# Gated linear attention with its features on the partitions: decays, queries and keys come out of TensorE unturned, and the state is kept at the middle of each tile

## The chip, the cores and the metric

The kernel runs on one core of a Trainium2 chip. The metric is the device time of one execution in microseconds (us). Instructions run on five engines that each work through their own queue in order: TensorE (PE in the profile), VectorE (DVE), ScalarE (ACT), GpSimd (POOL) and SyncE (SP, which issues most transfers). They wait for each other through semaphores.

## The reference, cut to what matters

The program computes two blocks on 512 tokens of width 1024. The first block, of two layers, is the one that the change touches. Its layer projects the normalized input to everything that two attentions need, runs both, gates them and projects back:

```python
z = rmsnorm(x, norm_g[l]) @ w_in[l]
(g_q, g_k, g_v, g_lr, g_gate, c_q, c_kv, k_pe, m_gate) = split(z)
log_a = log_sigmoid(g_lr @ w_gla_gate_up[l] + b_gla_gate[l]) / 16     # 512 x 4 heads x 64
# gated linear attention, 4 heads, keys of 64 features, values of 128, chunks of 64 tokens
b = cumsum(log_a within the chunk)
q_dec, k_inv = q * 64**-0.5 * exp(b), k * exp(-b)
o = tril(q_dec @ k_inv.T) @ v + q_dec @ state
state = exp(b_last) * state + (k * exp(b_last - b)).T @ v
o_gla = rmsnorm(o) * silu(g_gate)
# o_mla: causal softmax attention of 4 heads, queries and keys of 128 + 64 (rotated) features
x = x + concat(o_gla, o_mla * silu(m_gate)) @ w_out[l]
```

The second block (another mixer and a feed-forward part) is not touched.

## The kernel before, in words

All of the state fits on the chip: 512 tokens are four tiles of 128, `t` = 0 to 3, and the input `u` lies with its features on the partitions. A large projection is a chain of 24 matmuls of 512 columns, three for each of eight slices of 128 features (`mm3`, L232 to L234: each operand is split into a high and a low part, and high by high, high by low and low by high are added). The splits of the weights are a ScalarE cast (L94) and a VectorE subtraction (L95). Small matmuls and transposes are in float32; such a matmul has two records in the trace, a transpose one.

A layer of the first block runs in this order: a narrow projection (latent queries and keys, gate inputs) with `post_a`, `post_b`, `post_c` behind it, tile by tile; `queries` and `decays` (the log gates `la`); `keys`; `attention`; `output`. Between these steps stand calls of `fill`. A `Fill` holds a list of generators, each a large projection cut into pieces of 12 matmuls: the values (`vfill`), then queries and keys of the linear attention, then the two gates. One call issues the next piece on TensorE and then runs what was put off with `later(d, fn)` for d calls. The fill calls are thus what keeps TensorE busy while VectorE, ScalarE and GpSimd work on small things, and the order of the calls sets the order of every engine's queue.

The linear attention of a tile goes through `gla_decay` (cumulative sums of `la` as two float32 matmuls of 256 columns, L611 and L612, chunk ends in L621, then exponentials), `gla_qk` (the projected tile, tokens on the partitions, times the exponentials, L630 to L634), `gla_turn` (four transposes bring queries and keys to features on the partitions, copied in L644; then the update of the state, L656, added in L663 on VectorE, and the state at the tile's middle by one GpSimd multiplication, L649), `gla_scores` (L674) and `gla_out` (L688, L694), each one fill call after the other. The two 64-row halves of L674, L694 and L724 are pairs whose matmuls stand side by side in TensorE's array.

Behind `gla_out` comes a normalization: ScalarE squares the result in its PSUM banks (L699), VectorE sums (L700) and adds the epsilon (L701), GpSimd takes the power of -1/2 (L246), and VectorE multiplies out of PSUM (L706, tile `og`). Only then are the two PSUM tiles free. They come from the pool `"s"` of three buffers, from which `gla_scores`, `gla_out`, `mla_scores` (L721, L724, two tiles for two heads) and `keys` take theirs in turn; `"z"` has two (projections), `"tr"` two (transposes and state updates), `"o"` one.

Of the kernel before, what the change touches and what calls it, by code (L numbers as in the profile page):

```python
# [18 lines left out]
P = 128  # L19
# [153 lines left out]
class Layer:  # L173


    def __init__(self):
        self.fill = Fill()
        self.rqs, self.gexp, self.state = [], {}, None
        self.o, self.th, self.parts, self.ready, self.lat = {}, {}, {}, set(), {}
        self.scored = False  # L180
        self.oz = []


class K:
# [102 lines left out]
    def later_constants(self):  # L287
# [3 lines left out]
        c = cst.tile([P, 4 * P + 3], F32, name="c128")  # L291
# [3 lines left out]
        self.u_cum = c[:, P:2 * P]  # L295
        self.u_suf = c[:, 2 * P:3 * P]
        self.cmask = c[:, 3 * P:4 * P]
        self.ones = c[:, 4 * P:4 * P + 1]
# [207 lines left out]
    def decays(self, L):  # L506

        nc = self.nc
        ex = self.big([P, NT, 256])
        for t in range(NT):  # L510
# [8 lines left out]
        nc.vector.tensor_tensor(L.la[:], L.la[:], ex[:], ALU.subtract)  # L519
# [45 lines left out]
    def keys(self, L, wkv, t):  # L565
# [5 lines left out]
        for b in range(2):  # L571
            z = self.psum("o" if b and t % 2 else "s")
# [35 lines left out]
    def gla_decay(self, L, t):  # L608
        nc = self.nc
        psb = self.psum("s")  # L610
        nc.tensor.matmul(psb[:, 0:256], self.u_cum, L.la[:, t, :], start=True, stop=True)  # L611
        nc.tensor.matmul(psb[:, 256:512], self.u_suf, L.la[:, t, :], start=True, stop=True)  # L612
        e = self.lay.tile([P, 3, 256], F32, tag="gexp", name=self.name("gexp"))
        nc.scalar.activation(e[:, 0, :], psb[:, 0:256], AF.Exp)
        nc.scalar.activation(e[:, 1, :], psb[:, 0:256], AF.Exp, scale=-1.0)
        nc.scalar.activation(e[:, 2, :], psb[:, 256:512], AF.Exp)
        L.gexp[t] = e
        if t:
            pd = self.psum("tr", (P, 2, 256))
            for pr in range(2):  # L620
                nc.tensor.matmul(pd[:, pr, 0:2], L.la[:, t, pr * P:(pr + 1) * P], self.ends,  # L621
                                 start=pr == 0, stop=pr == 1)
            nc.scalar.activation(L.dec[:, t, :, :], pd[:, :, 0:2], AF.Exp)

    def gla_qk(self, L, t, z):
        nc = self.nc
        e, r = L.gexp.pop(t), L.r
        q_ = self.t2()
        ke = self.lay.tile([P, 256], F32, tag="ke", name=self.name("ke"), bufs=2)
        nc.vector.scalar_tensor_tensor(q_[:, 0:256], z[:, 0:256], L.r8[:, t:t + 1], e[:, 0, :],  # L630
                                       ALU.mult, ALU.mult)
        nc.vector.scalar_tensor_tensor(q_[:, 256:512], z[:, 256:512], r[:, t:t + 1], e[:, 1, :],
                                       ALU.mult, ALU.mult)
        nc.vector.scalar_tensor_tensor(ke[:], z[:, 256:512], r[:, t:t + 1], e[:, 2, :],  # L634
                                       ALU.mult, ALU.mult)
        L.fill.later(1, lambda: self.gla_turn(L, t, q_, ke))

    def gla_turn(self, L, t, q_, ke):
        nc = self.nc
        pst = self.psum("tr", (P, 4, P))  # L640
        for c in range(4):
            self.transpose(pst[:, c, :], q_[:, c * P:(c + 1) * P])
        qkT = self.lay.tile([P, 4, P], F32, tag="qkT", name=self.name("qkT"), bufs=2)
        nc.scalar.copy(qkT[:], pst[:])  # L644

        st = None
        if t:
            st = self.lay.tile([P, 2, P], F32, tag="mid", name=self.name("mid"), bufs=2)
            nc.gpsimd.tensor_tensor(st[:], L.state[:],  # L649
                                    L.dec[:, t, :, 0:1].to_broadcast([P, 2, P]), ALU.mult)  # L650
        if t < NT - 1:
            pu = self.psum("tr", (P, 2, P))
            for i in range(2):
                for par in range(2):
                    h = 2 * i + par
                    nc.tensor.matmul(pu[64 * par:64 * par + 64, i, :], ke[:, h * 64:(h + 1) * 64],  # L656
                                     L.v[:, t, h * P:(h + 1) * P], start=True, stop=True)
            if t == 0:
                L.state = self.lay.tile([P, 2, P], F32, tag="state", name=self.name("st"))
                nc.vector.tensor_copy(L.state[:], pu[:])  # L660
            else:
                for pr in range(2):
                    nc.vector.scalar_tensor_tensor(L.state[:, pr, :], L.state[:, pr, :],  # L663
                                                   L.dec[:, t, pr, 1:2], pu[:, pr, :],
                                                   ALU.mult, ALU.add)
        L.fill.later(1, lambda: self.gla_scores(L, t, qkT, st))

    def gla_scores(self, L, t, qkT, st):
        nc = self.nc
# [10 lines left out]
        L.fill.later(1, lambda: self.gla_out(L, t, qkT, st))  # L680

    def gla_out(self, L, t, qkT, st):
        nc = self.nc
        po = [self.psum("s", (P, 4, P)), self.psum("s", (P, 4, P))]
        for i in range(2):
# [4 lines left out]
        if st is not None:  # L690
            for i in range(2):
                for par in range(2):
                    b = slice(64 * par, 64 * par + 64)
                    nc.tensor.matmul(po[par][:, i, :], qkT[b, i, :], st[b, i, :],  # L694
                                     start=False, stop=i == 1)
        og = self.lay.tile([P, 4, P], F32, tag="o", name=self.name("og"), bufs=4)
# [153 lines left out]
    def layer(self, l):  # L850
# [11 lines left out]
        L.la = self.lay.tile([P, NT, 256], F32, tag="la", name=self.name("la"))  # L862
# [58 lines left out]
        L.r8, L.rh = self.sm(NT), self.sm(NT)  # L921
        nc.vector.tensor_scalar(L.r8[:], L.r[:], GLA_DK ** -0.5, None, ALU.mult)
# [12 lines left out]
        fill()  # L935
        for t in range(1, NT):
# [4 lines left out]
        L.dec = self.lay.tile([P, NT, 2, 2], F32, tag="dec", name=self.name("dec"))  # L941
        fill.add(self.tok_fill(T, lambda t, z: self.gla_qk(L, t, z),
                               lambda t: self.gla_decay(L, t)))
# [746 lines left out]
def _shape_constants():  # L1690
# [3 lines left out]
    suf = np.where(upto, 0.0, 1.0 / 16.0)  # L1694
    ends = np.stack([mid / 16.0, np.full(P, 1.0 / 16.0)], 1)
# [62 lines left out]
```

## Time and profile before

| | us |
|---|---|
| median of 3 runs | 1280.02 (1279.86 to 1280.14) |
| the profiled execution | 1280.23 |
| its span in the trace | 1278.5 |
| TensorE busy | 1261.9 (99%) |
| VectorE busy | 706.8 (55%) |
| ScalarE busy | 517.2 (40%) |
| GpSimd busy | 210.7 (16%) |

The span is what the trace covers, from the first to the last instruction; the 1.7 us around it belong to the execution and not to any engine. Busy time of TensorE counts overlapping matmuls once and their modelled ends with them, so that work is better read from one start to the next.

### The profile page before, as it was taken

The page shows a single profiled execution, that of the slowest core. Times are in us where ns is not written, and L with a number is a line of the kernel's source. Part 1 is how long each engine was busy: PE and PEld are TensorE (multiplying, and loading weights), DVE is VectorE, ACT ScalarE, POOL GpSimd, SP SyncE. Part 2 cuts the span into 40 slices and gives each one's busy share as a digit, 9 for nine tenths or more (in the row PEclk, how much of TensorE's full clock was granted, in tenths as well). Part 3 has the DMA queues.
Part 4 walks back from the last instruction along what each step waited for, and adds up shares of the span by engine and source line. Part 5 has one row for each costly group of instructions (what it writes and reads, how often), then busy time and mean ns, then how long its engine had stood idle before and what let it go on. Part 6 is the DMA issues. An engine that isn't in the chain of part 4 may idle for free.

```text
span 1278.5 us, 16438 instructions
## 1 busy us (share of the span) xinstructions
PE 1261.9 (99%) x6218; PEld 1031.4 (81%) x6218; DVE 706.8 (55%) x1310; ACT 517.2 (40%) x1174; POOL 210.7 (16%) x239
## 2 busy tenths in 40 slices
PE   8999999999999999999999999999999999999997
PEld 6877778888777888888888888887888888888886
DVE  8667555566556464555376447646655533555532
ACT  6654334356334352225643334445433222333231
POOL 4442001344200230000010002200311100111110
PEclk9999999999999999999999999999999999999999
DMA  6223014513112365222123323323323224333311
GB/s 225 63 99 102 28 39 146 174 46 99 53 64 67 112 221 194 75 92 66 63 78 100 95 95 107 101 98 99 99 90 93 74 87 128 106 98 95 110 44 66
DMA packets 39392, 124.40 MB, mean 97 GB/s; under 512 B 4812, under 2 KB 5862, under 8 KB 39184
## 3 DMA queue, kind: packets, MB, share of 16 engines
q1 hardware_dynamic: 36432, 114.18, 27.7%
q0 software_dynamic: 2592, 8.86, 2.2%
q8 instruction: 49, 0.80, 0.3%
q10 hardware_dynamic: 288, 0.31, 0.1%
q14 instruction: 31, 0.25, 0.1%
HBM read 117.04 MB, written 6.29 MB: 96 GB/s over the span
## 4 chain that ended last, share of the span: by engine, by line
PE 92%; DVE 3%; ACT 2%; issue 1%; DMA 1%; POOL 0%; SPq 0%; POOLq 0%; DVEq 0%; ACTq 0%
PE psz L232 24%; PE psz L233 23%; PE psz L234 23%; PE pstr L241 4%; PE pss L232 3%; PE pss L234 3%; PE pss L233 3%; PE pss L721 1%; PE pso L758 1%; PE pss L724 1%; DVE wlo L95 1%; PE pss L1458 1%; PE pss L1125 1%; PE pss L674 0%; PE pso L1257 0%
## 5 line engine op out<-in xcount | busy, mean ns | idle before, releaser
L94 ACT CAST whi<-wraw 128x512 fp32r<-128x512 f32 (+4 forms) x420 | 227.0, 595 | 316.1 <-PE psz L233 214.5
L95 DVE TENSOR_TENSOR wlo<-wraw,whi 128x512 fp32r<-128x512 f32 (+4 forms) x420 | 300.4, 757 | 89.8 <-ACT whi L94 89.1
L232 PE MATMUL psz<-u,whi 128*128 128x512 f32 x640 | 251.0, 392 | 0.0
L234 PE MATMUL psz<-u,wlo 128*128 128x512 f32 x640 | 249.4, 390 | 0.0
L233 PE MATMUL psz<-u,whi 128*128 128x512 f32 x640 | 249.4, 390 | 0.0
L232 PEld LDWEIGHTS psz<-u,whi 128*128 128x128 f32 x640 | 120.2, 188 | 25.5 <-issue 0.7
L234 PEld LDWEIGHTS psz<-u,wlo 128*128 128x128 f32 x640 | 120.2, 188 | 25.2
L233 PEld LDWEIGHTS psz<-u,whi 128*128 128x128 f32 x640 | 120.2, 188 | 24.2
L232 PE MATMUL psz<-whi,u 128*128 128x512 f32 (+1 forms) x320 | 128.4, 401 | 0.0
L232 PE MATMUL psz<-big,whi 128*128 128x512 f32 (+1 forms) x328 | 126.0, 384 | 0.1
L234 PE MATMUL psz<-big,wlo 128*128 128x512 f32 (+1 forms) x328 | 124.9, 381 | 0.0
L233 PE MATMUL psz<-big,whi 128*128 128x512 f32 (+1 forms) x328 | 124.8, 380 | 0.0
L234 PE MATMUL psz<-whi,u 128*128 128x512 f32 (+1 forms) x320 | 122.9, 384 | 0.0
L233 PE MATMUL psz<-wlo,u 128*128 128x512 f32 (+1 forms) x320 | 122.9, 384 | 0.0
L1538 POOL TENSOR_TENSOR t<-t,t 128x512 f32<-128x512 f32 x22 | 34.4, 1561 | 255.2 <-DVE t L1536 242.7
L232 PEld LDWEIGHTS psz<-whi,u 128*128 128x128 f32 x320 | 60.7, 190 | 17.6 <-issue 7.2
L370 POOL TENSOR_TENSOR t<-t,t 128x512 f32<-128x512 f32 x35 | 49.0, 1399 | 151.6 <-ACT t L369 151.2
L232 PEld LDWEIGHTS psz<-big,whi 128*128 128x128 f32 x328 | 61.6, 188 | 12.9 <-DVE x L994 0.5
L234 PEld LDWEIGHTS psz<-big,wlo 128*128 128x128 f32 x328 | 61.6, 188 | 12.4
L233 PEld LDWEIGHTS psz<-big,whi 128*128 128x128 f32 x328 | 61.6, 188 | 12.2 <-issue 0.2
L234 PEld LDWEIGHTS psz<-whi,u 128*128 128x128 f32 x320 | 60.7, 190 | 12.0
L233 PEld LDWEIGHTS psz<-wlo,u 128*128 128x128 f32 x320 | 60.8, 190 | 9.8 <-issue 0.3
(366 smaller groups left out, 1849.1 us busy)
## 6 DMA issues: line engine op xcount, KB each, us to landing
wraw<-wts SPq DMA_DIRECT2D x166, 512.0 KB, 4.2
wraw<-wts SPq DMA_DIRECT2D x16, 384.0 KB, 3.2
wraw<-wts SPq DMA_DIRECT2D x16, 352.0 KB, 3.1
x<-t SPq DMA_DIRECT2D x16, 256.0 KB, 4.3
big<-xT SPq DMA_DIRECT2D x8, 256.0 KB, 5.1
t<-xT POOLq DMA_DIRECT2D x8, 256.0 KB, 3.5
t<-x POOLq DMA_DIRECT2D x8, 256.0 KB, 4.6
x<-x SPq DMA_DIRECT2D x8, 256.0 KB, 3.1
```

The lines of the kernel that those rows point to most:

```text
L94: nc.scalar.copy(hi, raw)
L95: nc.vector.tensor_tensor(lo, raw, hi.bitcast(F32), ALU.subtract)
L232: mm(out, lhsT[0], rhs[0], start=start, stop=False)
L233: mm(out, lhsT[0], rhs[1], start=False, stop=False)
L234: mm(out, lhsT[1], rhs[0], start=False, stop=stop)
L241: self.nc.tensor.transpose(out, in_, self.ident[0:n, 0:n])
L370: nc.gpsimd.tensor_tensor(self.sq[:], self.sq[:], s[:], ALU.add)
L721: nc.tensor.matmul(s[:, 0:n], L.qT[:, h, ts], L.kT[:, h, 0:n], start=True, stop=False)
L724: nc.tensor.matmul(s[:, 0:n], L.rT[b, hp, ts], L.rT[b, 2 + hp, 0:n], start=False, stop=True)
L758: nc.tensor.matmul(L.po[:, h, :], pT[:, j, :], L.vm[:, j, h * P:(h + 1) * P], start=j == 0, stop=j == t)
L1125: nc.tensor.matmul(dst, qk[b, i, tsl[tt]], qk[b, 2 + i, kc], start=True, stop=True)
L1538: nc.gpsimd.tensor_tensor(gt[:], gt[:], up[:], ALU.mult)
```

## The change

The decays are made with features on the partitions from the start: `gla_decay` multiplies `la` (now the stationary operand) by the matrix of cumulative sums and two more columns, 130 columns, for two pairs of heads, and writes the exponentials straight into `L.qk`, which holds queries (0, 1) and keys (2, 3) for all 512 tokens. It is called in the loop over `queries`. The projection of queries and keys is turned round too (`feat_fill2`: weights stationary, `u` streaming, as many matmuls as before), and `gla_qk` multiplies each of its four results by `R`, the input's norm factor broadcast to all partitions, and by the decay. Queries and keys need no transposes for the scores then; the keys alone are transposed back, two transposes for each tile but the last, for the state's update. All four tiles' scores, output and update now follow the last of the four results. The update is added to the state and multiplied by one factor, so that the state is always the one at a tile's middle. Beside this, `decays` subtracts tile by tile, the keys of the second attention take their PSUM tiles from `"s"` alone, `gate_weights(0)` is called after the first projection, and the first layer's `fill(2)` before `post_b` is `fill()`.

The diff, cut:

```diff
@@ later_constants
-        self.u_cum = c[:, P:2 * P]
-        self.u_suf = c[:, 2 * P:3 * P]
-        self.ends = c[:, 4 * P + 1:4 * P + 3]
+        self.cum = c[:, P:2 * P + 2]
-        self.gate_weights(0)
@@ decays
-        nc.vector.tensor_tensor(L.la[:], L.la[:], ex[:], ALU.subtract)
+        for t in range(NT):
+            nc.vector.tensor_tensor(L.la[:, t, :], L.la[:, t, :], ex[:, t, :], ALU.subtract)
@@ keys
-            z = self.psum("o" if b and t % 2 else "s")
+            z = self.psum("s")
@@ gla_decay (the old body, gla_qk and gla_turn are removed)
+        ps = self.psum("o", (P, 2, 256))
+        for pr in range(2):
+            nc.tensor.matmul(ps[:, pr, 0:P + 2], L.la[:, t, pr * P:(pr + 1) * P], self.cum,
+                             start=True, stop=True)
+        nc.scalar.activation(L.qk[:, 0:2, ts], ps[:, :, 0:P], AF.Exp)
+        nc.scalar.activation(L.qk[:, 2:4, ts], ps[:, :, 0:P], AF.Exp, scale=-1.0)
+        nc.vector.tensor_copy(L.halves[:, t], ps[:, :, P:P + 2])
+            nc.vector.tensor_tensor(L.dec[:, t, :], L.halves[:, t - 1, :, 1], L.halves[:, t, :, 0],
+                                    ALU.add)
+            nc.scalar.activation(L.dec[:, t, :], L.dec[:, t, :], AF.Exp)
+    def gla_qk(self, L, m, z):
+        zr = self.t2()
+        if m < 2:
+            nc.vector.scalar_tensor_tensor(zr[:], z[:], GLA_DK ** -0.5, L.R[:], ALU.mult, ALU.mult)
+        else:
+            nc.vector.tensor_tensor(zr[:], z[:], L.R[:], ALU.mult)
+        (nc.vector if m == 3 else nc.gpsimd).tensor_tensor(L.qk[:, m, :], zr[:], L.qk[:, m, :],
+                                                           ALU.mult)
+        if m == 3:
+            L.fill.later(1, lambda: self.gla_scores(L, 0))
@@ gla_scores
-                nc.tensor.matmul(pas[par][:, i, :], qkT[b, 2 + i, :], qkT[b, i, :],
+                nc.tensor.matmul(pas[par][:, i, :], L.qk[b, 2 + i, ts], L.qk[b, i, ts],
+        if t < NT - 1:
+            pst = self.psum("tr", (P, 2, P))
+            for pr in range(2):
+                self.transpose(pst[:, pr, :], L.qk[:, 2 + pr, ts])
+            kt = self.lay.tile([P, 256], F32, tag="ke", name=self.name("ke"))
+            nc.scalar.copy(kt[:].rearrange("p (a c) -> p a c", a=2), pst[:])
+        L.fill.later(1, lambda: self.gla_out(L, t, kt))
@@ gla_out (between the output's matmuls and its normalization)
+        if kt is not None:
+            pu = self.psum("tr", (P, 2, P))
+            for i in range(2):
+                for par in range(2):
+                    h = 2 * i + par
+                    nc.tensor.matmul(pu[64 * par:64 * par + 64, i, :], kt[:, h * 64:(h + 1) * 64],
+                                     L.v[:, t, h * P:(h + 1) * P], start=True, stop=True)
+            new = self.lay.tile([P, 2, P], F32, tag="mid", name=self.name("mid"), bufs=2)
+            for pr in range(2):
+                d = L.dec[:, t + 1, pr:pr + 1]
+                if st is None:
+                    nc.vector.tensor_scalar(new[:, pr, :], pu[:, pr, :], d, None, ALU.mult)
+                else:
+                    nc.vector.tensor_tensor(new[:, pr, :], pu[:, pr, :], st[:, pr, :], ALU.add)
+                    nc.gpsimd.tensor_scalar(new[:, pr, :], new[:, pr, :], d, None, ALU.mult)
+            L.mid = new
+            L.fill.later(1, lambda: self.gla_scores(L, t + 1))
@@ layer, l == 0
             roots()
+            self.gate_weights(0)
...
             fill.add(vfill)
-            fill(2)
+            fill()
@@ layer
         for t in range(1, NT):
             self.queries(L, wq, t)
+            self.gla_decay(L, t - 1)
             fill()
+        self.gla_decay(L, NT - 1)
+        L.R = self.t2()
+        self.r_bcast(L.r, L.R[:])
-        fill.add(self.tok_fill(T, lambda t, z: self.gla_qk(L, t, z),
-                               lambda t: self.gla_decay(L, t)))
+        rhs = [self.u(k, slice(0, T)) for k in range(KD)]
+        fill.add(self.feat_fill2(rhs, lambda m, z: self.gla_qk(L, m, z)))
```

`r_bcast` is four float32 matmuls of 128 columns and one ScalarE copy.

How the queues change at two places. On TensorE in the first layer, before, from the last matmuls of tile 1's output (L694) on; `pss` is a PSUM tile of pool `"s"`, `psz` one of a large projection:

```order
L694 MATMUL pss202_1225<-mid180_1119,qkT179_1117 128x128
L694 MATMUL pss203_1226<-mid180_1119,qkT179_1117 128x128
L241 MATMUL pstr208_1244<-c128_233,t2_198_1210 128x128 x4
L656 MATMUL pstr211_1253<-big52_436,ke199_1211 64x128 x4
L611 MATMUL pss212_1260<-la10_126,c128_233 128x256
L612 MATMUL pss212_1260<-la10_126,c128_233 128x256
L621 MATMUL pstr214_1267<-c128_233,la10_126 128x2 x2
L232 MATMUL psz215_1271<-whi6_877,u17_159 128x512
L233 MATMUL psz215_1271<-wlo6_878,u17_159 128x512
L234 MATMUL psz215_1271<-whi6_877,u19_161 128x512
```

Nine more projection matmuls follow there, and then L674, the scores of the next tile, which take the PSUM tiles that the output leaves. At the same place in the changed kernel (its lines: L672 is the output's last part, L680 the state's update, L717 and L720 the scores of the softmax attention):

```order
L672 MATMUL pss220_1363<-mid197_1279,qk88_676 128x128
L672 MATMUL pss221_1364<-mid197_1279,qk88_676 128x128
L680 MATMUL pstr222_1373<-big51_435,ke212_1335 64x128 x4
L717 MATMUL pss228_1392<-big131_877,big68_586 128x256
L720 MATMUL pss228_1392<-big69_587 128x256
L232 MATMUL psz219_1350<-whi9_1227,u17_159 128x512
L233 MATMUL psz219_1350<-wlo9_1228,u17_159 128x512
L234 MATMUL psz219_1350<-whi9_1227,u19_161 128x512
L232 MATMUL psz219_1350<-whi9_1227,u17_159 128x512
L233 MATMUL psz219_1350<-wlo9_1228,u17_159 128x512
L717 MATMUL pss229_1393<-big131_877,big68_586 128x256
L720 MATMUL pss229_1393<-big69_587 128x256
```

The third tile of the pool (228) goes to the first head of `mla_scores`; the second head's (229) is the buffer of 220, the output's first tile. The two heads, adjacent in the program, are pulled apart by projection matmuls.

On GpSimd in the first layer, before, at the end of its work for the linear attention (`sm` is a root of a normalization, `mid` the state at a tile's middle):

```order
L246 TENSOR_TENSOR sm_1238<-sm_1237,mhalf 128x4
L649 TENSOR_TENSOR mid_1356<-st_984,dec_852 128x256
L246 TENSOR_TENSOR sm_1343<-sm_1342,mhalf 128x4
L246 TENSOR_TENSOR sm_1458<-sm_1457,mhalf 128x4
L960 DMA t_365_2081<-xT 128x512
```

In the changed kernel the same stretch reads:

```order
L631 TENSOR_TENSOR qk_676<-t_177_1154,qk_676 128x512
L246 TENSOR_TENSOR sm_1285<-sm_1284,mhalf 128x4
L689 TENSOR_SCALAR mid_1378<-mid_1378,dec_678 128x128 x2
L246 TENSOR_TENSOR sm_1386<-sm_1385,mhalf 128x4
L689 TENSOR_SCALAR mid_1488<-mid_1488,dec_678 128x128 x2
L246 TENSOR_TENSOR sm_1496<-sm_1495,mhalf 128x4
L246 TENSOR_TENSOR sm_1595<-sm_1594,mhalf 128x4
```

The state's two multiplications stand ahead of the root of the same tile's output, for tiles 1 and 2.

## Rows read from the trace of the kernel before

**Rows 1.** The page's chain of waits: share of the span by engine.

```profile
PE 92%; DVE 3%; ACT 2%; issue 1%; DMA 1%; POOL 0%; SPq 0%; POOLq 0%; DVEq 0%; ACTq 0%
```

**Rows 2.** TensorE's waits: line waited at, releaser, us in total, times, longest.

```profile
PE pss L234 <- DVE u L364: 1.4, 1, 1.4
PE pstr L241 <- ACT big L602: 1.0, 1, 1.0
...
PE pstr L241 <- DVE sm L543: 0.7, 1, 0.7
PE pstr L241 <- DVE t L537: 0.7, 1, 0.7
```

**Rows 3.** Busy time by stretch: PE, PEld, DVE, ACT, POOL, granted clock, DMA.

```profile
126.50:130.00 3.50, 3.50 (x10) 2.76 (x10) 0.78 (x4) 1.01 (x4) 0.00 (x0) 0.51 0.04 16
```

**Rows 4.** Timeline of TensorE, layer 1, tile 2: start, duration, engine, line, operation.

```profile
338.43 0.39 PE L234 MATMUL psz<-whi,u 128*128 128x512 f32 x1
...
340.03 1.05 PE L688 MATMUL pss<-big,AT 128*128 128x128 f32 x8
...
341.65 0.66 PE L241 MATMUL pstr<-c,t 128*128 128x128 f32 x4
342.24 0.66 PE L656 MATMUL pstr<-big,ke 128*64 128x128 f32 x8
342.83 0.70 PE L611 MATMUL pss<-la,c 128*128 128x256 f32 x2
...
343.79 0.50 PE L621 MATMUL pstr<-c,la 128*128 128x2 f32 x4
344.16 0.48 PE L232 MATMUL psz<-whi,u 128*128 128x512 f32 x1
```

**Rows 5.** Timeline of TensorE at two scores of the softmax attention, layer 0.

```profile
113.06 0.49 PE L721 MATMUL pss<-big,big 128*128 128x128 f32 x2
...
113.48 0.49 PE L724 MATMUL pss<-big 64*128 64x128 f32 x2
...
113.89 0.50 PE L232 MATMUL psz<-whi,u 128*128 128x512 f32 x1
...
136.76 0.70 PE L724 MATMUL pss<-big 64*128 64x256 f32 x4
137.39 0.50 PE L232 MATMUL psz<-whi,u 128*128 128x512 f32 x1
```

**Rows 6.** Timeline of all engines behind the output of tile 1, layer 0.

```profile
106.99 0.65 PE L241 MATMUL pstr<-c,t 128*128 128x128 f32 x4
107.09 0.66 ACT L699 ACTIVATE t<-pss 128x256 f32<-128x256 f32 x2 [1.07 <-PE pss L694]
...
107.78 0.69 DVE L700 TENSOR_REDUCE sm<-t 128x4 f32<-128x512 f32 x1 [0.49 <-ACT t L699]
...
108.38 0.34 DVE L663 SCALAR_TENSOR_TENSOR st<-st,dec,pstr 128x128 f32<-128x128 f32 x1
...
108.89 1.03 POOL L246 TENSOR_TENSOR sm<-sm,mhalf 128x4 f32<-128x4 f32 x1 [4.86 <-DVE sm L701]
...
109.95 0.76 DVE L706 TENSOR_TENSOR og<-pss,sm 128x256 f32<-128x256 f32 x2 [0.90 <-POOL sm L246]
...
110.41 0.61 POOL L649 TENSOR_TENSOR mid<-st,dec 128x256 f32<-128x256 f32 x1 [0.49 <-DVE og L706]
```

**Rows 7.** The same stretch of tile 2: first matmul behind the output, then the wait.

```profile
119.23 0.49 PE L232 MATMUL psz<-whi,u 128*128 128x512 f32 x1
...
124.16 0.60 PE L674 MATMUL pss<-qkT 64*128 64x128 f32 x3 [0.32 <-DVE og L706]
```

**Rows 8.** Timeline of VectorE and TensorE around the latent projection of layer 0.

```profile
16.80 1.46 DVE L265 TENSOR_TENSOR wgu<-t,wgu 32x256 fp32r<-32x256 f32 x1
...
38.92 0.47 DVE L492 SCALAR_TENSOR_TENSOR t<-pss,sm,rows 128x256 f32<-128x256 f32 x1
...
40.79 0.38 PE L241 MATMUL pstr<-c,t 128*65 128x128 f32 x2
```

More of the change, by code (lines that the diff above doesn't have):

```diff
@@ L177, in __init__ @@
         self.fill = Fill()
-        self.rqs, self.gexp, self.state = [], {}, None
+        self.rqs, self.state, self.mid = [], None, None
         self.o, self.th, self.parts, self.ready, self.lat = {}, {}, {}, set(), {}
@@ L290, in later_constants @@
         nc, I, cst = self.nc, self.I, self.cst
-        c = cst.tile([P, 4 * P + 3], F32, name="c128")
+        c = cst.tile([P, 3 * P + 3], F32, name="c128")
         nc.gpsimd.tensor_copy(c[:, 0:1], self.sq[:, 0:1])
@@ L294, in later_constants @@
         self.ident = c[:, 0:P]
-        self.u_cum = c[:, P:2 * P]
-        self.u_suf = c[:, 2 * P:3 * P]
-        self.cmask = c[:, 3 * P:4 * P]
-        self.ones = c[:, 4 * P:4 * P + 1]
-        self.ends = c[:, 4 * P + 1:4 * P + 3]
+        self.cum = c[:, P:2 * P + 2]
+        self.cmask = c[:, 2 * P + 2:3 * P + 2]
+        self.ones = c[:, 3 * P + 2:3 * P + 3]
         nc.gpsimd.tensor_copy(self.row[:, 0:1], self.sq[:, 0:1])
         nc.gpsimd.dma_start(self.row[:], I["rows"][0:1, :].partition_broadcast(P))
-        self.gate_weights(0)
         self.amask = self.const("amask", [P, P], I["amask"], I32)
@@ L509, in decays @@
         ex = self.big([P, NT, 256])
+        L.la = self.big([P, NT, 256])
         for t in range(NT):
@@ L609, in gla_decay @@
         nc = self.nc
[L610 to L616, printed above, removed]
@@ L617, in gla_decay @@
-        L.gexp[t] = e
-        if t:
[L619 to L625, printed above, removed]
-        nc = self.nc
[L627 to L636, printed above, removed]
@@ L638, in gla_turn @@
-    def gla_turn(self, L, t, q_, ke):
-        nc = self.nc
[L640 to L666, printed above, removed]
@@ L668, in gla_scores @@
-    def gla_scores(self, L, t, qkT, st):
-        nc = self.nc
+        ts = slice(t * P, (t + 1) * P)
+        ps = self.psum("o", (P, 2, 256))
[5 more added lines that the diff above has]
+        nc.vector.tensor_copy(L.halves[:, t], ps[:, :, P:P + 2])
@@ L670, in gla_scores @@
+    def gla_scores(self, L, t):
+        nc = self.nc
+        ts = slice(t * P, (t + 1) * P)
         pas = [self.psum("s", (P, 4, P)) for _ in range(2)]
@@ L679, in gla_scores, with gla_out @@
                                       pas[par][:, 0:2, :])
-        L.fill.later(1, lambda: self.gla_out(L, t, qkT, st))
-    def gla_out(self, L, t, qkT, st):
+        kt = None
+        if t < NT - 1:
[5 more added lines that the diff above has]
+        L.fill.later(1, lambda: self.gla_out(L, t, kt))
+    def gla_out(self, L, t, kt):
         nc = self.nc
+        ts = slice(t * P, (t + 1) * P)
         po = [self.psum("s", (P, 4, P)), self.psum("s", (P, 4, P))]
+        st = L.mid
         for i in range(2):
@@ L935, in layer @@
         fill()
+        L.qk = self.lay.tile([P, 4, T], F32, tag="qk", name=self.name("qk"))
+        L.halves = self.lay.tile([P, NT, 2, 2], F32, tag="halves", name=self.name("halves"))
+        L.dec = self.lay.tile([P, NT, 2], F32, tag="dec", name=self.name("dec"))
         for t in range(1, NT):
             self.queries(L, wq, t)
+            self.gla_decay(L, t - 1)
             fill()
+        self.gla_decay(L, NT - 1)
+        L.R = self.t2()
+        self.r_bcast(L.r, L.R[:])
         L.kT, L.vm = self.big(), self.big()
         (wkv,) = W.get(1, T, ahead=0)
[L941 to L943 removed]
+        rhs = [self.u(k, slice(0, T)) for k in range(KD)]
+        fill.add(self.feat_fill2(rhs, lambda m, z: self.gla_qk(L, m, z)))
         fill.add(self.tok_fill(T, lambda t, z: self.gate(L, "g", t, z)))
@@ L1693, in _shape_constants @@
     cum = (upto * 1.0 - mid[:, None] * 1.0) / 16.0
-    suf = np.where(upto, 0.0, 1.0 / 16.0)
-    ends = np.stack([mid / 16.0, np.full(P, 1.0 / 16.0)], 1)
+    halves = np.stack([mid / 16.0, (1.0 - mid) / 16.0], 1)
     cmask = np.where(i[None, :] <= i[:, None], 0.0, NEG)
     ifr = np.float32(10000.0) ** (-np.arange(0, ROPE, 2, dtype=np.float32) / np.float32(ROPE))
-    c128 = np.concatenate([np.eye(P), cum, suf, cmask, np.ones((P, 1)), ends],
+    c128 = np.concatenate([np.eye(P), cum, halves, cmask, np.ones((P, 1))],
                           1).astype(np.float32)
```

6 lines of the change are left out of this document (2 added, 4 removed).

## The prediction

> **What bounds the kernel now.** I read the page's chain of waits first: 92% of the time it lies on TensorE, 3% on VectorE, 2% on ScalarE [rows 1]. So a microsecond of TensorE's work taken away is a microsecond of the program, unless a wait fills it. Next the list of TensorE's own waits: each occurs once or twice, none is over about 2 us, and those near the change are short (the reader is to see 1.4, 1.0, 0.7 and 0.7 [rows 2]). Work that leaves VectorE, ScalarE or GpSimd is worth nothing by itself; what counts is TensorE's matmuls, and which of the other engines' chains become longer than the matmuls that cover them. Third, the timelines of the linear attention, for both.
>
> **TensorE's work.** Starts are compared with starts. In layer 1 seven projection matmuls take 340.03 - 338.43 = 1.60, 0.229 each [rows 4]. Tile 2's removed and kept small matmuls stand there in one block: 344.16 - 341.65 = 2.51, of which L656 (kept) is 342.83 - 342.24 = 0.59 and the chunk ends 344.16 - 343.79 = 0.37 [rows 4]. So a tile loses 1.92, tile 0 (no ends) 1.55; two layers with three and one: 6 x 1.92 + 2 x 1.55 = 14.6. Added are, for each of eight tiles, two float32 matmuls of 130 columns. The trace has none; the nearest is L656, as many streamed columns with its gap, 0.59, and four records of L621 with no columns to speak of still take 0.37; I take 0.55, near the first, 4.4 in all. Six pairs of transposes at half the 0.59 of four (342.24 - 341.65) are 1.8, and two broadcasts of R at no more than the same 0.59 are 1.2. Sum: 7.4 - 14.6 = -7.2, between -8.6 (decays at 0.37) and -6.2. The turned projection streams as many columns and I cost it at nothing, within 0.5 either way.
>
> One thing gives part of this back. The order shows the two heads of a `mla_scores` pulled apart at four places in each layer, where before there are two, at 128 columns. A 64-row half alone takes what the pair takes, because the pair runs side by side: a single one of 128 columns is 113.89 - 113.48 = 0.41, a pair of 256 is 137.39 - 136.76 = 0.63 [rows 5]; by the same step 384 is 0.84. The new places have 128, 256, 256 and 384 columns in layer 0 and 256, 256, 384, 384 in layer 1: 2.5 + 2.9, less 4 x 0.41 before, +3.8. The two places where `gla_scores` was pulled apart by a projection are gone: -0.8. Net +3.0, between 0 and +4.
>
> **The wait that the change makes.** Behind each `gla_out` the second head's scores write into the first PSUM tile of the output, so TensorE waits there for `og` (L706), at eight places. Queued behind it on TensorE is everything: the rest of the scores, projections, the next tile. Before, the tile is wanted again only behind 12 projections or more, and even so the one slow chain ended in a wait of 0.32 [rows 7].
>
> What the chain takes: from 106.99, the end of the output, squares, sum, epsilon, power, product, to 109.95 and half of 0.76, 110.33: 3.35 with one state addition (L663, 0.34) between [rows 6]. After the change VectorE does two such operations there (+0.35: 3.7), and for tiles 1 and 2 GpSimd must also do two multiplications of 128 x 128 ahead of the power. L649 has the same number of elements and takes 0.61 [rows 6]; the first begins when the first addition is through, some 1.7 behind the output's end, the second ends at about 2.6, the power starts there and not at 1.9 to 2.2: 4.15. Tile 3 has no update, but four casts ahead of its sum on VectorE: 3.9. The ends: 3.35 (all of it beside other work) and 4.93 (124.16 - 119.23, the slow one [rows 7]).
>
> What covers it (matmuls of the order, at the prices above): tile 0 0.59 + 0.83 + 7 x 0.229 = 3.0; tiles 1 and 2 0.59 + 1.05 + 5 x 0.229 = 2.8 (3.0 in layer 1's tile 2); tile 3 1.5 + 9 x 0.229 = 3.6. Waits: 0.7, 1.35, 1.35, 0.35 and 0.7, 1.35, 1.1, 0.35: 7.2. Ends: with 3.35 throughout about 2.6; with 4.93 throughout about 14.5.
>
> **The smaller edits.**
> - `fill()` for `fill(2)`: the first transposes of `post_c` come 12 x 0.229 = 2.75 earlier, at 38.05 instead of 40.79; one of them needs the latent of tile 0, ready at 38.92 + 0.47 = 39.39 [rows 8]. A lone projection lies between, so a wait of +1.0 (0 to 1.3).
> - `gate_weights` leaves VectorE's queue in the first projection, where its subtraction took 1.46 [rows 8], ahead of the input that TensorE then waits 1.4 for [rows 2]. GpSimd's additions set that pace too, so half of the wait goes: -0.65 (0 to -1.4).
> - Queries: two waits of 0.7 [rows 2] get the 12 projections that moved and the new decays as cover: -0.7 (0 to -1.4). If the decays' exponentials hold up ScalarE's copies there, nothing goes.
> - Keys: all four pairs now use three `"s"` tiles, and a pair can wait for the scaling of the pair before; the cover is 15 projections, 3.4, against a chain of the same five steps as behind the output, 3.35 to 4.93 [rows 6, 7]; with the new first output, which has two projections between scores and itself, +0.5 (0 to +3).
> - The wait of 1.0 for L602 [rows 2] falls into the old tile 0's block: -0.6 (0 to -1.0). The slow chain's 0.3: -0.3.
> - The clock. From 126.5 to 130.0 the granted clock was 0.51, the lower level, 1.2 GHz; ten matmuls ran there [rows 3]. In front of it stood a stretch of short float32 matmuls with a wait. That stretch is rebuilt: it costs 3.5 x 0.49 = 1.7, and I book -1.2 (-1.7, or more drops, below).
> - VectorE loses twelve small products a layer and gains eight large ones; the four subtractions in `decays` replace one: nothing, as they lie beside projections.
>
> **Sum.** -7.2 + 3.0 + 7.2 + 1.0 - 0.65 - 0.7 + 0.5 - 0.6 - 0.3 - 1.2 = +1.05. On the profiled execution that is 1280.23 + 1.05 = 1281.3, and that one stands 0.2 above the median of the runs: 1281.1.
>
> **The rivals.**
> 1. *The chain fits.* VectorE's two additions slip in while it waits for the squares (it stands idle there for 0.49 [rows 6]), GpSimd's multiplications are done before the epsilon. Then the waits are 2.6 and not 7.2: 1276.5, and with the keys and `post_c` hidden too, 1275. For it: before, one addition already fits into 3.35. Against: the update's matmuls come between the output and the additions, 0.59 late.
> 2. *GpSimd is slow in the chain*, and it ends slower: at the eight places the multiplications and the power are stretched as in the chain of tile 2, which took 4.93 for 3.35 [rows 7]. From 4.15 to 4.93 at four places and 3.8 to 4.93 at the others is 3 + 4.5 = +7.5: 1288 to 1289. It decides from a chain of 4.5 on (+3). Against: in the order no casts stand between these VectorE operations, as they did in tile 2's.
> 3. *The clock drops at the new waits.* Eight waits beside short float32 matmuls are as many places like the one in front of 126.5 [rows 3]. Four drops would be 4 x 1.7 + 1.2 = +8: 1289. Against: the wait of 1.0 in layer 1 [rows 2] is in a like stretch and no drop follows it.
>
> The Trainium skill (TensorE: Matmul & The Clock Gate, "A second HAM failure mode: psum-queue depth-cycling") says that a kernel whose TensorE pauses briefly and often between groups of matmuls, waiting for PSUM buffers, can swing between the two clocks, and loses by that more than the pauses. It speaks for rival 3, since these are waits for PSUM; the row of 126.5 agrees that small pauses can be enough, the one of 1.0 us does not.
>
> **How the numbers follow.** Forecast 0.45, 1278 to 1284.5 by its own terms; rival 1 0.30; rival 2 0.17; rival 3 0.08. 0.2%, 2.6 us, is about what a measurement of this kernel tells from no change. Of the forecast some 0.34 lies within that, 0.09 above and 0.02 below; of rival 1 0.28 is below. So faster 0.30, no change 0.36, slower 0.34. The range takes in most of rival 1 and the lower end of rival 2: 1274 to 1287.
>
> **What would show it.** Right: in the waits of TensorE a row of L717 (the scores of the softmax attention) behind VectorE's `og`, eight times, 6 to 9 us in all and none over 2; a wait of about 1 before the first `post_c`; small matmuls of the decays and transposes at some 7 us less than before; no stretch at half clock between 70 and 215. Wrong: no such row (rival 1), that row at over 12 (rival 2), granted clocks of a half in several stretches (rival 3), or waits at places that I have at nothing, above all in the queries or where the turned results are multiplied.

## The result, and the profile after

The changed kernel takes 1288.27 us (median of 4 runs, 1287.58 to 1288.63) against 1279.94 beside it: ratio 1.0069, 95% interval 1.0055 to 1.0084. It is 0.7% slower. The prediction, 1281.1 in a range of 1274 to 1287, was too low, and the time lies outside the range. The profiled execution took 1288.00, with a span of 1286.3, 7.8 more than before.

TensorE's list of waits, with the columns of [rows 2], shows new rows near the top (a row reads: line waited at, releaser, us in total, times, longest):

```profile
PE pss L717 <- DVE og L702: 5.3, 5, 1.4
PE pss L233 <- DVE wlo L95: 3.2, 3, 1.7
PE pstr L241 <- DVE t L489: 2.6, 1, 2.6
PE pso L613 <- DVE big L518: 1.4, 1, 1.4
PE pstr L241 <- DVE t L589: 1.4, 2, 0.7
...
PE pso L613 <- DVE halves L617: 0.9, 1, 0.9
...
PE pss L717 <- DVE sm L731: 0.5, 2, 0.3
PE pss L232 <- ACT t L576: 0.5, 1, 0.5
```

The first is the wait for the normalized output that the prediction named. The second, for a split of the weights, is not new (2.5 before). The third is the one before the first `post_c`, and it is not 1.0 but 2.6. The others stand in the queries (L613), the keys (L589, L576) and the scores (L717 for L731); the four rows of [rows 2] are gone.

By the landmarks that both traces have (the starts of the input's norm sums, of `decays` and of the next layer), the first layer's norm sums come 1.1 earlier than before, the stretch from there to `decays` is 1.7 longer, the rest of layer 0 is 4.4 longer, layer 1 is 2.7 longer, and everything behind is as long as it was (790).

The stretches of 3.5 us, columns as in [rows 3], at the first `post_c` and at the place where the clock fell before:

```profile
39.50:43.00 3.50, 2.90 (x9) 2.36 (x10) 2.96 (x11) 1.91 (x8) 1.36 (x2) 0.59 0.55 187
...
126.50:130.00 3.50, 3.35 (x21) 1.87 (x17) 1.45 (x5) 0.66 (x2) 1.66 (x3) 1.00 0.00 0
```

In these two profiles the lower clock has moved from the attention to the stretch right behind the wait of 2.6. The seven projections from 40.38 to 43.30 start 0.42 to 0.64 apart there, where 0.229 is usual.

All engines behind the output of tile 1, layer 0, the answer to [rows 6]:

```profile
126.56 0.66 PE L680 MATMUL pstr<-big,ke 128*64 128x128 f32 x8
126.67 0.66 ACT L695 ACTIVATE t<-pss 128x256 f32<-128x256 f32 x2 [3.93 <-PE pss L672]
...
127.36 0.69 DVE L696 TENSOR_REDUCE sm<-t 128x4 f32<-128x512 f32 x1 [2.20 <-ACT t L695]
...
127.96 0.48 DVE L688 TENSOR_TENSOR mid<-pstr,mid 128x128 f32<-128x128 f32 x2
128.34 1.24 POOL L689 TENSOR_SCALAR mid<-mid,dec 128x128 f32<-128x128 f32 x2 [9.86 <-DVE mid L688]
128.35 0.16 DVE L697 TENSOR_SCALAR sm<-sm 128x4 f32<-128x4 f32 x1
...
129.46 0.40 PE L233 MATMUL psz<-wlo,u 128*128 128x512 f32 x1
129.56 1.03 POOL L246 TENSOR_TENSOR sm<-sm,mhalf 128x4 f32<-128x4 f32 x1
130.62 0.42 DVE L702 TENSOR_TENSOR og<-pss,sm 128x256 f32<-128x256 f32 x1 [1.81 <-POOL sm L246]
...
131.19 0.67 PE L717 MATMUL pss<-big,big 128*128 128x256 f32 x2 [1.33 <-DVE og L702]
```

The sum with its epsilon is done at 128.51, but the power starts at 129.56, because GpSimd's two multiplications (1.24) stand ahead of it. From the output's end to the product it is 131.04 - 126.56 = 4.5 (3.35 before, 4.15 expected).

The decays' matmuls and the broadcast in layer 1, to be read against [rows 4]:

```profile
304.50 0.61 PE L613 MATMUL pso<-c,big 128*128 128x130 f32 x4
304.95 1.05 PE L390 MATMUL pss<-c,sm 128*128 128x128 f32 x8
305.76 0.48 PE L232 MATMUL pss<-whi,big 128*128 128x512 f32 x1
```

Two matmuls of 130 columns take 0.45, the broadcast 0.81.

### The profile page after: what moved, and what is told of

Same layout as the page of the kernel before. It is cut to its first block, busy times and chain, and to the rows that moved or that the text cites. A ratio compares the mean times of both kernels' runs of the same rounds, so it can differ in the third digit from the quotient of the medians.

```text
span 1286.3 us, 16389 instructions
## 1 busy us (share of the span) xinstructions
PE 1260.4 (98%) x6190; PEld 1024.2 (80%) x6190; DVE 704.8 (55%) x1316; ACT 514.9 (40%) x1166; POOL 218.4 (17%) x247
## 4 chain that ended last, share of the span: by engine, by line
PE 65%; DVE 2%; issue 1%; ACT 0%; POOL 0%; POOLq 0%; ACTq 0%; DVEq 0%
PE psz L232 19%; PE psz L234 19%; PE psz L233 19%; PE pstr L241 2%; PE pss L232 1%; PE pss L234 1%; PE pss L233 1%; PE pss L1459 1%; PE pss L1126 1%; PE pso L754 0%; PE pso L1258 0%; PE pss L717 0%; PE psz L1498 0%; POOL sm L246 0%; PE pss L1498 0%
## 5 line engine op out<-in xcount | busy, mean ns | idle before, releaser
L232 PE MATMUL psz<-u,whi 128*128 128x512 f32 x704 | 276.8, 393 | 0.0
L234 PE MATMUL psz<-u,wlo 128*128 128x512 f32 x704 | 274.5, 390 | 0.0
L233 PE MATMUL psz<-u,whi 128*128 128x512 f32 x704 | 274.3, 390 | 0.0
L232 PEld LDWEIGHTS psz<-u,whi 128*128 128x128 f32 x704 | 132.2, 188 | 28.0 <-issue 0.7
L234 PEld LDWEIGHTS psz<-u,wlo 128*128 128x128 f32 x704 | 132.2, 188 | 27.9
L233 PEld LDWEIGHTS psz<-u,whi 128*128 128x128 f32 x704 | 132.2, 188 | 26.8
L232 PE MATMUL psz<-whi,u 128*128 128x512 f32 (+1 forms) x256 | 102.3, 400 | 0.0
L234 PE MATMUL psz<-whi,u 128*128 128x512 f32 (+1 forms) x256 | 98.2, 384 | 0.0
L233 PE MATMUL psz<-wlo,u 128*128 128x512 f32 (+1 forms) x256 | 98.2, 383 | 0.0
L246 POOL TENSOR_TENSOR sm<-sm,mhalf 128x4 f32<-128x4 f32 (+2 forms) x38 | 35.0, 921 | 168.5 <-DVE sm L697 51.3
L232 PEld LDWEIGHTS psz<-whi,u 128*128 128x128 f32 x256 | 48.6, 190 | 15.6 <-issue 9.0
L234 PEld LDWEIGHTS psz<-whi,u 128*128 128x128 f32 x256 | 48.7, 190 | 10.2 <-issue 1.2
```

The costliest lines, as they stand in the source:

```text
L232: mm(out, lhsT[0], rhs[0], start=start, stop=False)
L233: mm(out, lhsT[0], rhs[1], start=False, stop=False)
L234: mm(out, lhsT[1], rhs[0], start=False, stop=stop)
L246: self.nc.gpsimd.tensor_tensor(out, a, self.mhalf[:, 0:n], ALU.pow)
```

## The experiments

Ratios are to the kernel before, run beside each on the same chip, with 95% intervals. Kernels of one group shared those runs.

**e1_fill2**: the changed kernel with the 12 projections back before `post_b`.

```diff
             fill.add(vfill)
-            fill()
+            fill(2)
```

> The changed kernel with fill(2) back in layer 0, nothing else. Theory: the wait of 2.64 us before the first post_c and the stretch at half clock right behind it (granted 0.59 from 39.5 to 43.0, about 1.9 us lost) come from the missing 12 projections. Then 12 projections (2.75 us) cover the wait, the wait falls to under 0.3 us, no half clock there, and the time falls by 3.5 to 4.5 us, to about 1284. Rival: the 12 projections are missing as cover in the queries afterwards (waits for the decays there grow from 2.3 us) and give most of it back: 1286 to 1288.

Measured 1285.84, ratio 1.0044 (1.0030 to 1.0057); span 1282.4, 3.9 under the changed kernel's. The wait for L489 is gone from the list and the stretch runs at the full clock:

```profile
39.50:43.00 3.50, 3.50 (x20) 2.84 (x19) 3.35 (x13) 1.63 (x7) 1.00 (x2) 1.00 0.42 150
```

In the spans the theory holds; the medians, from two groups of runs, differ by 2.4, and the ratios by 3.2. The rival falls: the queries now wait 1.4 for L536 (0 in the changed kernel), but the two rows of the decays (L613) fall by as much, from 2.3 to 0.9.

**e2_out_tr**: the changed kernel with the output's second PSUM tile from another pool.

```diff
-        po = [self.psum("s", (P, 4, P)), self.psum("s", (P, 4, P))]
+        po = [self.psum("s", (P, 4, P)), self.psum("tr", (P, 4, P))]
```

> The changed kernel with the second PSUM tile of gla_out taken from pool tr in place of s. The two heads of the softmax scores then stand side by side again and need no tile of the output. Theory (the PSUM pool of three makes the waits and the split pairs): waits for og go from 5.3 us to under 1, the scores' matmuls (L717, L720) lose about 4.5 us, the time falls by 7 to 10 us, to 1278 to 1281. Rival (the time went into the first layer's start and the queries): the time falls by under 3 us, and the transposes wait for og in their turn.

Measured 1278.49, ratio 0.9984 (0.9976 to 0.9993); span 1276.8, 9.5 under the changed kernel's. One word turns the change from slower to faster. The same place as above, now with the two heads side by side and without a wait:

```profile
124.66 0.66 PE L680 MATMUL pstr<-big,ke 128*64 128x128 f32 x8
125.25 1.13 PE L717 MATMUL pss<-big,big 128*128 128x256 f32 x4
126.31 0.70 PE L720 MATMUL pss<-big 64*128 64x256 f32 x4
126.95 0.50 PE L232 MATMUL psz<-whi,u 128*128 128x512 f32 x1
```

Summed from start to start over both layers, and without the stretch at the lower clock that this profile also has, L717 and L720 lose 6.7. The 512-column projections lose about 1.0: ten fewer follow another kind of matmul, and the first one behind such a seam takes 0.31 in place of 0.23. The waits for `og` are gone, but new ones take the place of some:

```profile
PE pstr L241 <- ACT t L746: 3.2, 4, 1.2
...
PE pstr L241 <- ACT ke L655: 1.0, 2, 0.5
```

So 7.7 is the pulled-apart pairs with their seams and 3.4 the waits (counted from where the next matmul was due), less 1.8 by which other small matmuls are longer: 9.3 of the 9.5.

**e3_start_only**: the kernel before with the two edits of the start.

```diff
-        self.gate_weights(0)
...
             roots()
+            self.gate_weights(0)
...
-            fill(2)
+            fill()
```

> The kernel before with only two edits of the change: gate_weights(0) behind the first projection, and fill() for fill(2). Theory: the start of the first layer is slower by itself: first projection 1.1 us shorter, then a wait of 2 to 3 us before the first post_c and a stretch at half clock; but the 12 projections come back as cover in the queries, where before has 2.2 us of waits. Time 1280 to 1283. Rival: with nothing of the rest changed the waits in the queries vanish altogether, time 1278 to 1279.5.

Measured 1279.33, ratio 0.9991 (0.9982 to 0.9999): no slower than before, and in the rival's range. The theory's wait before `post_c` is there, but no stretch at the lower clock behind it, and the one at 126.5 is gone too; the queries' two waits of 0.7 went, as the rival said:

```profile
PE pstr L241 <- DVE t L491: 2.8, 1, 2.8
...
39.50:43.00 3.50, 2.66 (x13) 2.24 (x14) 3.48 (x13) 2.13 (x10) 1.60 (x3) 1.00 0.57 203
```

The same wait thus does or doesn't bring the lower clock. In the five profiles with a wait of 2.4 to 2.8 there it came in three (the changed kernel, e2_out_tr, e4_scale_last) and not in two (e3_start_only, e13_scale_dve).

**e4_scale_last**: the state's multiplications written behind the power.

```diff
-                    nc.gpsimd.tensor_scalar(new[:, pr, :], new[:, pr, :], d, None, ALU.mult)
...
         self.rsqrt(r4[:], s4[:])
+        if kt is not None and st is not None:
+            for pr in range(2):
+                nc.gpsimd.tensor_scalar(new[:, pr, :], new[:, pr, :], L.dec[:, t + 1, pr:pr + 1],
+                                        None, ALU.mult)
```

> The changed kernel with GpSimd's two multiplications of the state issued behind the power of the output's root instead of ahead of it (tiles 1 and 2 of both layers). Theory that they lengthen the chain to og: the four waits of tiles 1 and 2 shrink by 0.4 to 0.7 us each, time lower by 1.5 to 2.8 us, about 1286. Rival, that the multiplications lie beside VectorE's sum: no change beyond 0.5 us.

Measured 1287.71, ratio 1.0060 (1.0047 to 1.0072). It tells nothing of the chain: the order of the queue isn't that of the code, and the multiplications (now L700) still run ahead of the power.

```profile
127.30 1.25 POOL L700 TENSOR_SCALAR mid<-mid,dec 128x128 f32<-128x128 f32 x2 [9.85 <-DVE mid L688]
...
128.52 1.03 POOL L246 TENSOR_TENSOR sm<-sm,mhalf 128x4 f32<-128x4 f32 x1
```

Its profile shows something else. The clock fell a second time, right behind a wait for `og` in the attention, at the place where the changed kernel waited 1.33 and kept the full clock. The scores that waited, and the stretch behind them (columns as in [rows 3]):

```profile
130.15 0.67 PE L720 MATMUL pss<-big,big 128*128 128x256 f32 x2 [1.36 <-DVE og L705]
```

```profile
131.80:135.20 3.40, 3.40 (x11) 2.39 (x9) 0.58 (x2) 1.33 (x3) 0.00 (x0) 0.50 0.00 0
```

**e13_scale_dve** asked it again: the multiplications on VectorE.

```diff
-                    nc.gpsimd.tensor_scalar(new[:, pr, :], new[:, pr, :], d, None, ALU.mult)
+                    nc.vector.tensor_scalar(new[:, pr, :], new[:, pr, :], d, None, ALU.mult)
```

> The changed kernel with the state's two multiplications (tiles 1 and 2 of both layers) on VectorE in place of GpSimd. In the changed kernel the two stand on GpSimd for 1.24 us ahead of the power (128.34 to 129.56), which could have begun at 128.5. Theory: the chain to og gets about 0.7 us shorter at four places; two more projections stand in the order between the heads there (0.46); the four waits go from 5.1 to under 1.5 us, the time falls by 2.5 to 4, to 1284.5 to 1286. Rival: VectorE's two additional operations lie in the same chain and cost what GpSimd's did: under 1 us.

Measured 1282.72, ratio 1.0012 (1.0002 to 1.0023); span 1280.5, 5.8 under the changed kernel's. The rival falls: 1.24 on GpSimd became 0.47 on VectorE, and the power starts with the sum.

```profile
126.82 0.47 DVE L689 TENSOR_SCALAR mid<-mid,dec 128x128 f32<-128x128 f32 x2
127.21 0.16 DVE L697 TENSOR_SCALAR sm<-sm 128x4 f32<-128x4 f32 x1
127.45 1.01 POOL L246 TENSOR_TENSOR sm<-sm,mhalf 128x4 f32<-128x4 f32 x1 [10.51 <-DVE sm L697]
128.49 0.42 DVE L702 TENSOR_TENSOR og<-pss,sm 128x256 f32<-128x256 f32 x1 [0.92 <-POOL sm L246]
129.06 0.67 PE L717 MATMUL pss<-big,big 128*128 128x256 f32 x2 [0.30 <-DVE og L702]
```

The row of waits for `og` falls from 5.3 to 1.5. By the landmarks the stretches behind `decays` of layer 0 and behind the norm sums of layer 1 are 2.4 and 1.8 shorter; the remaining 1.5 lies between the first norm sums and `decays`, where this profile has no stretch at the lower clock, and isn't the edit's.

**e10_lone_halves** priced a pulled-apart pair by itself, in a kernel (e5_both, below) where all pairs stand together.

```diff
             nc.tensor.matmul(s[:, 0:n], L.qT[:, h, ts], L.kT[:, h, 0:n], start=True, stop=False)
-        for par, s in enumerate(ss):
             b = slice(64 * par, 64 * par + 64)
```

> As e5_both, but in all 16 scores of the softmax attention the 64-row half of each head follows its own 128-row part, so that no two halves stand side by side; no wait or buffer is changed. Theory (a lone half takes what the pair takes): 0.42, 0.63, 0.84, 1.05 us more for 128, 256, 384, 512 columns, four times each: 11.8 us more than e5_both, 1288. Rival (what a pulled-apart pair costs is the change between kinds of matmul, about 0.1 us at each seam): 2 to 3 us more, 1279.

Measured 1285.03, ratio 1.0041 (1.0029 to 1.0054), against 0.9963 for e5_both. First a lone half of 384 columns, then the pair in e5_both:

```profile
159.67 0.91 PE L719 MATMUL pss<-big 64*128 64x384 f32 x2
160.51 0.91 PE L717 MATMUL pss<-big,big 128*128 128x384 f32 x2
```

```profile
160.58 0.92 PE L720 MATMUL pss<-big 64*128 64x384 f32 x4
161.43 0.50 PE L232 MATMUL psz<-whi,u 128*128 128x512 f32 x1
```

One half 0.84, both together 0.85. Over both layers the halves take 11.6 more (11.8 expected), and the 128-row parts, which follow each other no more, 3.2; 8.6 arrive in the median, because the longer scores cover 4.7 of TensorE's waits (counted from where the next matmul was due) `gla_scores` gives back 0.9, and the norm sums start 0.5 earlier. So the theory holds, and the rival's seams come on top. The Trainium skill (TensorE: Matmul & The Clock Gate, "Why this matters for your kernels") says that a matmul on part of the rows takes as long as a full one and that only running several at once gains; this trace agrees, with 0.84 for one half and 0.85 for two.

**e11_gate_early**: the changed kernel with `gate_weights(0)` at its old place.

```diff
+        self.gate_weights(0)
         self.amask = self.const("amask", [P, P], I["amask"], I32)
...
             roots()
-            self.gate_weights(0)
```

> The changed kernel with gate_weights(0) back at its old place, nothing else. Theory: the first projection's end is 1.1 us later again (a wait of 1.4 us for the input comes back) and the wait before the first post_c shorter by as much, since the latent's chain starts from transfers and not from TensorE: no change beyond 0.7 us. Rival: the chain follows TensorE, and the time is 1 us longer.

Measured 1285.84, ratio 1.0052 (1.0038 to 1.0065); span 1284.1, 2.2 under the changed kernel's. Neither theory nor rival: the input's norm sums start 0.9 later (1.1 expected), but in these two profiles the latent is ready 1.2 earlier, and the wait is 0.6 for 2.6. In the changed kernel and here the operation that makes it starts at:

```profile
39.48 0.47 DVE L489 SCALAR_TENSOR_TENSOR t<-pss,sm,rows 128x256 f32<-128x256 f32 x1
```

```profile
38.31 0.47 DVE L490 SCALAR_TENSOR_TENSOR t<-pss,sm,rows 128x256 f32<-128x256 f32 x1
```

How much of the 1.2 is the edit's is open. Over all 16 profiles this operation starts between 38.50 and 40.04 in the twelve with the moved `gate_weights` and between 38.31 and 39.82 in the four without, so the place of the call doesn't separate them; the intervals of the two ratios overlap too. What it does separate is TensorE: the norm sums start at 30.4 to 31.0 with the moved call and at 31.4 to 33.1 without. So TensorE came earlier and the latent did not come with it. What sets the latent's time is not shown.

This profile, too, has the lower clock in the attention, behind a wait for `og` of 1.31 that the changed kernel has as well, there without it:

```profile
143.90:147.30 3.40, 3.40 (x13) 2.41 (x11) 0.62 (x3) 1.34 (x3) 0.00 (x0) 0.50 0.00 0
```

**The repairs together.** e5_both is e1_fill2 and e2_out_tr in one; e6_decay_late and e7_keys_o each add an edit, e9_all both:

```diff
             self.queries(L, wq, t)
-            self.gla_decay(L, t - 1)
             fill()
+            self.gla_decay(L, t - 1)
```

```diff
-            z = self.psum("s")
+            z = self.psum("o" if b and t % 2 else "s")
```

> The changed kernel with both repairs: fill(2) in layer 0 and the output's second PSUM tile from pool tr. Theory (the start and the PSUM pool are separate losses, 3.9 and 9.4 us of the spans measured alone): they add, span 1286.3 - 13.3 = 1273, time 1274 to 1276, faster than the kernel before. Rival (the same matmuls are cover for both, so that the repairs eat each other): 1277 to 1279.

> As e5_both, with gla_decay(t - 1) called behind the loop's fill instead of ahead of it. Theory: the waits of the decays' matmuls (L613, for the subtraction of la and for the copy of the halves, 0.9 us with fill(2) back, 2.3 without) are there because the decays stand too early in the queries; 12 projections later they are gone: 0.5 to 1 us below e5_both. Rival: the waits move to the keys, no change.

> As e5_both, with the second PSUM tile of the keys of odd tiles from pool o again, as in the kernel before. Theory: the wait of the keys' transposes for the scaling (L241 behind L589, 1.4 us in two) and the one for ScalarE (L576, 0.5) come from three s tiles for four; 1 to 2 us below e5_both. Rival: they come from the order of VectorE's queue (the turned results' products among it), and stay: within 0.5 us.

> e5_both with the late decays of e6_decay_late and the keys' tile of e7_keys_o together. Theory: their gains (1.5 and 2.3 us below e5_both) lie at different places and add: 1272 to 1273.5. Rival: the decays at their later place take the o tile that the keys now wait for: no better than 1274.

Measured: e5_both 1276.46, 0.9963 (0.9951 to 0.9976); e6_decay_late 1274.92, 0.9955 (0.9943 to 0.9968); e7_keys_o 1274.20, 0.9950 (0.9936 to 0.9963); e9_all 1272.98, 0.9950 (0.9937 to 0.9962). The time of e5_both lies between theory and rival. By the ratios the two repairs add (0.0106 below the changed kernel, of 0.0025 and 0.0085); by the spans of single profiles e5_both is 2.0 under e2_out_tr, where `fill(2)` alone gave 3.9, and 0.5 of what is missing lies ahead of the norm sums, where the two programs are the same. In e7_keys_o the rows L589 (1.4) and L576 (0.5) are gone, which shows the pool as their cause; its median is 2.3 under e5_both's. In e6_decay_late the two L613 rows are gone, but L536 waits 1.6 for 0.3, so that the waits of 1.9 have mostly moved; its median is 1.5 under e5_both's, with intervals that overlap. e9_all is 1.2 under e7_keys_o in the median, from another group of runs, with the same ratio: no gain is shown.

**e8_before_tr**: the edit of e2_out_tr in the kernel before.

> The kernel before with one edit: the output's second PSUM tile from pool tr. Theory: in the kernel before, too, scores are pulled apart by the pool of three (4 heads, 4 x 0.41 us, and gla_scores in two places, 0.8 us) and one wait of 0.3 us is for it; 1 to 3 us below before, less than the 9.4 that the same edit gave in the changed kernel. Rival: the transposes and state updates in tr, which are more there, wait instead: no gain or slower.

Measured 1282.66, ratio 1.0021 (1.0012 to 1.0029): slower, and the rival is right. There, `tr` also serves the chunk ends, and four transposes for each tile where the changed kernel has two, and these wait in their turn. Of the 3.3 by which its span is longer, 1.4 lie ahead of the first norm sums, where this profile has a stretch at the lower clock (22.5 to 25.9) and the edit changes nothing; layer 1 is 2.2 longer.

```profile
PE pstr L621 <- DVE og L706: 1.5, 3, 0.6
...
PE pss L721 <- DVE og L706: 1.0, 2, 0.8
```

**e12_best** is e9_all with `gate_weights(0)` early, **e14_all_dve** e9_all with the multiplications on VectorE.

> e9_all with gate_weights(0) back at its old place as well. Theory: with fill(2) back the latent is waited for 0.2 us only, so that its being ready earlier is worth nothing, and the old place costs up to 0.8 us in the first projection: 1272.5 to 1274, no better than e9_all. Rival: the earlier casts help what follows the latent too: 1271 to 1272.

> e9_all with the state's multiplications on VectorE. Theory: with the output's second tile in tr nothing waits for the power at once any more; the transposes of the softmax attention wait for ScalarE (3.2 us) whatever GpSimd does: within 0.7 us of e9_all. Rival: those waits hang on og through tr, and 1 to 2 us go.

Measured 1274.44, ratio 0.9952 (0.9939 to 0.9966), for the first: no difference, as the theory said. The second took 1270.65, ratio 0.9922 (0.9905 to 0.9940), span 1270.0: 0.8% faster than the kernel before and the fastest of all. Its theory fell and the rival's size came: against e9_all the rows L746 and ke L655 lose 1.9, and the median, from another group of runs, is 2.3 lower.

```profile
PE pstr L241 <- ACT t L746: 2.3, 2, 1.2
```

## Why the prediction was wrong, point by point

By the spans the change cost 7.8 where the sum said 1.05. Sums of matmuls are from start to start, over both layers; waits are those of the list. Two steps failed, the start and the queries.

- *The small matmuls*, booked -7.2: right in sum. Removed are 7.1 (L611, L612), 2.2 (ends) and 4.0 (transposes), 13.3 for the 14.6 booked; added 3.4 (L613), 1.6 (L390) and 1.5 (transposes of the keys), 6.5 for 7.4: -6.8.
- *The pulled-apart pairs*, booked +3.0: right, and near in size. L717 and L720 take 4.8 more than L721 and L724 did, `gla_scores` 1.0 less: +3.8. Seams are no further term against the kernel before: 91 of the 512-column projections follow another kind of matmul, and 89 did.
- *The wait for* `og`, booked 7.2 at eight places with none over 2: the place and mechanism were right, 5.3 at five places and 0.5 at two, where VectorE's L731 ended last. At tiles 1 and 2 it is 5.1 for 5.15, but that is luck. The price of GpSimd's multiplications was too low (two take 1.24 and not the 0.61 that one of L649 for the same number of elements takes [rows 6]), so that the chain took 4.5 for 4.15; and the cover was priced too low by as much, for the next projection was due at 129.46 + 0.23, 3.1 behind the output's end, and not at 2.8. e13_scale_dve shows that 3.8 of the 5.3 hang on the multiplications.
- *The start*, booked +1.0 and -0.65: this step failed. It added the new wait and TensorE's earlier arrival as two separate terms. But the latent did not come earlier with TensorE: the norm sums started 1.1 earlier, the operation that makes the latent at 39.48 for 38.92 [rows 8]. So what TensorE gained went into the wait: 1.0, 1.1 and 0.56 are the 2.6 that it took. Behind it came the lower clock, about 1.6, for which the sum had nothing there. Together -1.1 + 2.6 + 1.6 = 3.1 for 0.35. e1_fill2, with the 12 projections back, has neither the wait nor the lower clock. In the kernel before the same two edits cost nothing (e3_start_only), because the 12 projections then cover the queries' waits; in the changed kernel the decays bring new waits there.
- *The queries*, booked -0.7: this step failed too, with the wrong sign. The old waits of 1.4 went, but the decays' matmuls (L613), whose waits were put at nothing, wait 1.4 for VectorE's subtraction in `decays` (L518) and 0.9 for its copy of the halves (L617): +0.9. e6_decay_late, with the decays later, has neither row, though another grew.
- *The keys*, booked +0.5 within 0 to 3: the mechanism was right, the size 1.9. e7_keys_o shows that they wait for the pool.
- *The clock*, booked -1.2: the stretch at 126.5 is at the full clock (-1.6), and another came, counted above. This is in part chance, since e3_start_only, with the attention of the kernel before, has no such stretch either.
- The waits of 1.0 and 0.3, booked -0.9, went whole: -1.3.

This gives -6.8 + 3.8 + 5.8 + 3.1 + 0.9 + 1.9 - 1.6 - 1.3 = +5.8 of 7.8. The list counts a wait from the modelled end of the matmul in front; counted from where the next matmul was due, the waits grew by 1.6 more. That makes 7.4; 0.4 stays open.

Rival 1 fell: the chain did not fit. Rival 2 had the sign and nearly the time (1288), and half of its reason: GpSimd was slow in the chain, but the chain reached 4.5, the point from which that rival decides, and not 4.93; the rest of its 7.5 came from the start, the queries and the keys, so that its time was met by luck. Rival 3 did not come in the changed kernel's profile: the granted clock is 1.00 at its waits for `og`, and fell once, behind a wait twice as long. But it isn't refuted. The changed kernel, e1_fill2, e4_scale_last and e11_gate_early each have four waits for `og` of 1.1 to 1.4, and behind two of these 16, one in e4_scale_last and one in e11_gate_early, the granted clock was 0.50. The Trainium skill (TensorE: Matmul & The Clock Gate, "A second HAM failure mode: psum-queue depth-cycling") says that frequent short pauses of TensorE between groups of matmuls that cycle through PSUM can make the clock swing. These two places agree with it, and the other 14 show that such a pause need not be enough.

## What to carry to other kernels

When a reordered stage shares a pool of PSUM tiles with another, list who takes the buffers in turn and what frees each: here the third of three buffers set both a wait and the order, and one tile from another pool was worth more (9.5) than the net work that was removed (6.8). Price an operation on GpSimd by itself and not by elements. When an edit lets TensorE come earlier, ask whether the chain that it will wait for comes earlier too: here the latent did not, and the gain became a wait. Do not book an earlier arrival and a wait behind it as separate terms.

## What was not expected of the hardware

- Two multiplications of 128 x 128 by a factor for each partition took 1.24 on GpSimd, one of 128 x 256 with a tensor 0.61; on VectorE the two took 0.47.
- The same wait of 2.4 to 2.8 in the same place was followed by the lower clock in three profiles and by the full clock in two; of 16 waits of 1.1 to 1.4 for `og`, two were followed by the lower clock.
